# Hybrid decoder layer on one Trainium2 core: smaller first pieces, state matmuls over 128 rows, and the gate's weight parts in one tile

## The chip, the cores and the metric

The kernel runs on one core of one Trainium2 chip. The metric is the device time of one execution in microseconds (us), lower is better. A core has five engines that run their own instruction streams: TensorE (PE in the profile; its weight loads are PEld), VectorE (DVE), ScalarE (ACT), GpSimd (POOL) and SyncE (SP). SP, ACT and POOL can issue DMA transfers, each on a queue of its own. A "q" behind an engine's name in a row means its sequencer, which issues DMAs.

## The reference

One decoder layer on x of 256 tokens by 2048 features, in float32, with three residual blocks:

```python
x = x + 0.5 * swiglu(rms_norm(x, ffn1_norm), w_gate, w_up, w_down)       # 2048 -> 5632 -> 2048
h = rms_norm(x, mix_norm);  z = h @ w_in                                 # columns split among head groups
# gated linear attention (GLA), 4 heads, dk 128, dv 256, chunks of 64 tokens:
log_a = log_sigmoid((g_low @ gla_gate_up) * ... + gla_gate_bias) / 16    # g_low: 16 columns of z
#   S_c = decay_c * S_{c-1} + k_state_c^T @ v_c ;  o_c = q_c S_{c-1} + masked scores @ v_c
# dilated attention, 8 heads of 128, three causal windows merged by their denominators
x = x + concat(o_gla, o_att) @ w_out
x = x + 0.5 * swiglu(rms_norm(x, ffn2_norm), ...)
```

With 256 tokens there are four chunks, so states after chunks 0, 1 and 2 are needed.

## The kernel before

**Arithmetic.** The large products run as three matmuls in fp32r. Every operand is split into a high part (a copy rounded to fp32r, on ACT, L89) and a low part (the rest, on DVE, L90) by `split`, and `products` sums high times high (L171), low weight times high (L173) and high weight times low (L175). Activations (`hh`/`hl`, 128 tokens at a time) are the stationary operand, the weights stream by as 128x512. The small matmuls of the two attentions run in plain fp32; each of them shows as two passes in the trace.

**Weights.** All weight matrices lie in DRAM as tiles of 128x2048 (1 MB). `prepare` takes the next entry of the list `jobs`: at even k it issues the 1 MB transfer into `raw` (three buffers) on SP's queue, the very first one in four pieces of 256 KB (L148), and then splits one 128x1024 half into `wh` and `wl` (four buffers each, `WBUF`). `weights` keeps up to three tiles prepared ahead of use. One such tile is used for 12 matmuls (two token halves, two column halves, three products). The special job "low" brings 128 columns of `w_in`, from the 16 gate columns on, and splits them into two pairs of `wh`/`wl`.

**Start.** `WARM` matmuls on a zeroed tile run on TensorE first (L78). `gT` (the norms' gains, 24 KB) is loaded on ACT's queue. `first(i)` loads two k-tiles of the transposed x (`xt`, 256 KB, ACT's queue, L259) into one of four `t512` buffers, and makes `hh` (ACT, L263) and `hl` (DVE, L264) of them. `first(0)` and `first(1)` are called before the first feed-forward block, the others from within its first column pair; the rms factor itself is applied later, when results leave PSUM.

**Column pairs.** `column_pair` runs over all k tiles of two 512-column blocks of outputs and calls pieces of other work from the list `later` in between. The tile framework orders each engine's instructions by a simulated schedule, so the program's order is a guide and not the exact order.

**GLA part.** `gate_low` multiplies the "low" tiles (stationary, 128x128 of which 16 columns matter) with `hh` and `hl` (256 tokens streaming): three matmuls for each of 16 k tiles (L441 to L443). Its 16 useful rows go to `gl`, and a matmul over 16 rows with `gup` (L450) gives the gate. `decays` and `scaled` make the decay factors `e1` to `e3` and scale q and k; the end of `scaled` multiplies `kg` by the decay to the end of the chunk (L485). `gla_head` makes for chunk c = 0, 1, 2 the state `kg^T @ vg` from the 64 rows (tokens) of the chunk (L521), adds the decayed state before (L527), and then the outputs with 64-column stationary operands (L536, L539).

Of the kernel before, what the change touches and what calls it, by code (L numbers as in the profile page):

```python
# [14 lines left out]
F32 = mybir.dt.float32  # L15
# [3 lines left out]
ALU = mybir.AluOpType  # L19
# [11 lines left out]
WARM = 7  # L31
# [5 lines left out]
def layer_kernel(tc, x, xT, gains, gla_gate_up, gla_gate_bias, gla_out_norm, att_q_norm, att_k_norm,  # L37
# [6 lines left out]
    with ExitStack() as es:  # L44
# [42 lines left out]
        def split(dst_h, dst_l, src):  # L87

            nc.scalar.activation(dst_h, src, AF.Copy)  # L89
            nc.vector.tensor_sub(dst_l, src, dst_h.bitcast(F32))  # L90
# [33 lines left out]
        def wtile(name):  # L124
            return wp.tile([P, 2, 512], F32R, name=name, tag=name, bufs=WBUF)

        def prepare():
            if not jobs:
                return
            job = jobs.pop(0)  # L130
            if job == "low":
                raw = wp.tile([P, KT, P], F32, name="raw", tag="raw", bufs=3)
                nc.sync.dma_start(raw, w_low.rearrange("p (k f) -> p k f", f=P))
                got = []
                for i in range(2):
                    wh, wl = (wtile(n).rearrange("p j f -> p (j f)").rearrange("p (k f) -> p k f", f=P) for n in ("wh", "wl"))
                    split(wh, wl, raw[:, 8 * i:8 * i + 8, :])
                    got.append((wh, wl))
                ready.extend(got)
                return  # L140
            w, i, k = job
            if k == 0:
                raw = raws[0] = wp.tile([P, 2, 2, 512], F32, name="raw", tag="raw", bufs=3)
                flat = raw.rearrange("p k j f -> p (k j f)")
                parts = 1 if started else 4
                started.append(True)
                for c in range(0, 2048, 2048 // parts):
                    nc.sync.dma_start(flat[:, c:c + 2048 // parts], w[i, :, c:c + 2048 // parts])  # L148
            wh, wl = wtile("wh"), wtile("wl")
            split(wh, wl, raws[0][:, k])  # L150
            ready.append((wh, wl))

        def weights():
            while jobs and len(ready) <= AHEAD:
                prepare()
            return ready.pop(0)
# [100 lines left out]
        def first(i):  # L257
            xt = t512("xt").rearrange("p (k s) -> p k s", k=2)
            nc.scalar.dma_start(xt, xTv[:, 2 * i:2 * i + 2, :])  # L259
# [22 lines left out]
        first(0)  # L282
        first(1)
# [3 lines left out]
        with tc.tile_pool(name="mix", bufs=1, reuse_waits="tile") as mp:  # L287
# [5 lines left out]
            gup = mp.tile([RANK, 512], F32, name="gup")  # L293
# [19 lines left out]
            ld(gup, gla_gate_up)  # L313
# [121 lines left out]
            def gate_low():  # L435
                gb = acc_bank()
                for k in range(KT):
                    if k % 8 == 0:
                        wh, wl = weights()
                    h, l = wh[:, k % 8, :], wl[:, k % 8, :]  # L440
                    nc.tensor.matmul(gb[:, :S], lhsT=h, rhs=hh[:, k, :], start=k == 0, stop=False)  # L441
                    nc.tensor.matmul(gb[:, :S], lhsT=h, rhs=hl[:, k, :], start=False, stop=False)  # L442
                    nc.tensor.matmul(gb[:, :S], lhsT=l, rhs=hh[:, k, :], start=False, stop=k == KT - 1)  # L443
                gbias = t512("gbias")
                ld(gbias, gla_gate_bias.unsqueeze(0).to_broadcast([P, 512]))
                gl = mp.tile([RANK, 3 * P], F32, name="gl", tag="sc", bufs=6)
                nc.vector.tensor_copy(gl[:, :S], gb[:RANK, :S])
# [25 lines left out]

            def scaled(t):
# [10 lines left out]
                nc.vector.tensor_mul(kg[:, t, :], kg[:, t, :], er)  # L485
# [29 lines left out]
            def gla_head(h):  # L515
                st = [None]
                bs = [tp_bank(), tp_bank()]
                for c in range(3):
                    rows = slice((c % 2) * 64, (c % 2) * 64 + 64)
                    kv = bs[c // 2][:, (c % 2) * GDV:(c % 2) * GDV + GDV]  # L520
                    nc.tensor.matmul(kv, lhsT=kg[rows, c // 2, h * P:(h + 1) * P],  # L521
                                     rhs=vgv[rows, c // 2, h * GDV:(h + 1) * GDV], start=True, stop=True)
# [134 lines left out]
```

## Time and profile before

| | |
|---|---|
| median of 3 runs | 1775.6 us (1775.47 to 1775.72) |
| the profiled execution | 1776.39 us, span 1774.5 us |
| TensorE busy | 1763.4 us (99%) |
| VectorE, ScalarE, GpSimd busy | 995.3 (56%), 839.4 (47%), 372.4 us (21%) |
| bytes read from HBM | 350.35 MB, 199 GB/s over the span |

The span runs from the first to the last instruction of the profiled execution; the execution's own time lies 1.9 us above it. Matmuls are pipelined and their ends are modelled, so times between matmuls are best read from start to start.

### The profile page before, as it was taken

To read this page: it belongs to the slowest core of one execution; us is meant where nothing else is said; L and a number is where in the kernel's file an instruction comes from. 1 tells how busy PE (TensorE), PEld (TensorE's weight loads), DVE (VectorE), ACT (ScalarE), POOL (GpSimd) and SP (SyncE) were. 2 spreads that over 40 slices of the span, in tenths; PEclk is the share of its full clock that TensorE was granted. 3 is DMA by queue.
4 is the path that set the end of the run, shared out by engine and by line. 5 is a ranking of instruction groups with operands and counts; after the bars stand their busy time and mean duration, and the time that the engine had idled before them with its cause. 6 is when DMAs were issued, how large, how long until landed. Compare 5 with 4: busy or idle time off the path is not lost.

```text
span 1774.5 us, 21587 instructions
## 1 busy us (share of the span) xinstructions
PE 1763.4 (99%) x8286; PEld 1534.8 (86%) x8286; DVE 995.3 (56%) x1042; ACT 839.4 (47%) x1012; POOL 372.4 (21%) x738
## 2 busy tenths in 40 slices
PE   8999999999999999999999999999999999999999
PEld 7888888888888888888887788888888888888887
DVE  5555555555554646566655666555555555544544
ACT  6444444444444544565753455444444444444442
POOL 0333343434400001011000000333333343410000
PEclk9999999999999999999999999999999999999999
DMA  8566666666555556555444455666565656565653
GB/s 332 206 223 210 218 215 216 212 222 223 208 211 201 201 194 208 210 191 196 166 166 146 149 197 196 209 218 216 211 221 207 224 207 224 204 220 207 221 212 119
DMA packets 74648, 365.43 MB, mean 206 GB/s; under 512 B 17168, under 2 KB 30480, under 8 KB 32304
## 3 DMA queue, kind: packets, MB, share of 16 engines
q1 hardware_dynamic: 48672, 348.15, 55.0%
q0 software_dynamic: 22976, 12.73, 2.5%
q10 hardware_dynamic: 2896, 3.17, 0.6%
q8 instruction: 65, 1.06, 0.2%
q14 instruction: 39, 0.32, 0.0%
HBM read 350.35 MB, written 2.10 MB: 199 GB/s over the span
## 4 chain that ended last, share of the span: by engine, by line
PE 99%; ACT 1%; DMA 0%; DVE 0%; issue 0%; ACTq 0%
PE acc L171 32%; PE acc L173 32%; PE acc L175 32%; PE tp L85 1%; PE tp L521 0%; DMA xt<-in_xT_dram 0%; PE tp L387 0%; PE tp L536 0%; PE tp L539 0%; ACT wh L89 0%; ACT L454 0%; PE acc L441 0%; PE acc L443 0%; PE acc L442 0%; PE tp L413 0%
## 5 line engine op out<-in xcount | busy, mean ns | idle before, releaser
L90 DVE TENSOR_TENSOR wl<-raw,wh 128x1024 fp32r<-128x1024 f32 x658 | 802.8, 1224 | 713.4 <-ACT wh L89 713.2
L89 ACT ACTIVATE wh<-raw 128x1024 fp32r<-128x1024 f32 x658 | 692.1, 1056 | 864.4 <-PE acc L175 852.0
L173 PE MATMUL acc<-wl,hh 128*128 128x512 f32 x1792 | 547.6, 381 | 0.0
L175 PE MATMUL acc<-wh,hl 128*128 128x512 f32 x1792 | 543.6, 380 | 0.0
L171 PE MATMUL acc<-wh,hh 128*128 128x512 f32 x1792 | 536.6, 381 | 4.7 <-ACT wh L89 4.7
L233 POOL DMA_DIRECT2D ur<-us x704 | 344.2, 497 | 576.3 <-ACT sg L225 431.8
L171 PEld LDWEIGHTS acc<-wh,hh 128*128 128x128 f32 x1792 | 338.6, 189 | 53.6 <-ACT wh L89 5.0
L173 PEld LDWEIGHTS acc<-wl,hh 128*128 128x128 f32 x1792 | 338.6, 189 | 49.5 <-issue 2.0
L175 PEld LDWEIGHTS acc<-wh,hl 128*128 128x128 f32 x1792 | 338.4, 189 | 49.7 <-issue 2.1
L173 PE MATMUL acc<-wl,uh 128*128 128x512 f32 x704 | 212.5, 379 | 0.0
L175 PE MATMUL acc<-wh,ul 128*128 128x512 f32 x704 | 211.8, 379 | 0.0
L171 PE MATMUL acc<-wh,uh 128*128 128x512 f32 x704 | 210.6, 379 | 0.0
L175 PEld LDWEIGHTS acc<-wh,ul 128*128 128x128 f32 x704 | 133.1, 189 | 18.9
L171 PEld LDWEIGHTS acc<-wh,uh 128*128 128x128 f32 x704 | 133.0, 189 | 18.9
L173 PEld LDWEIGHTS acc<-wl,uh 128*128 128x128 f32 x704 | 133.1, 189 | 18.7
L106 POOL TENSOR_TENSOR rs<-a,mhalf 128x4 f32<-128x4 f32 (+1 forms) x12 | 17.4, 1454 | 278.7 <-DVE a L337 278.7
L307 POOL DMA_DIRECT2D rope<-in_c_rope_dram x1 | 0.7, 747 | 209.2 <-PE acc L175 209.2
L226 DVE SCALAR_TENSOR_TENSOR u<-acc,rt,sg 128x512 f32<-128x512 f32 x44 | 32.7, 744 | 0.0
L230 DVE STREAM_TRANSPOSE us<-u 128x512 f32<-128x512 f32 x44 | 31.3, 711 | 1.5
L225 ACT ACTIVATE sg<-acc,rt 128x512 f32<-128x512 f32 x44 | 29.8, 678 | 0.6
L90 DVE TENSOR_TENSOR ul<-ur,uh 128x512 fp32r<-128x512 f32 x44 | 30.1, 683 | 0.0
L106 POOL TENSOR_TENSOR rt<-ssum,mhalf 128x1 f32<-128x1 f32 x6 | 3.9, 642 | 123.1 <-DVE ssum L110 123.0
(147 smaller groups left out, 601.1 us busy)
## 6 DMA issues: line engine op xcount, KB each, us to landing
raw<-in_w_ff_dram SPq DMA_DIRECT2D x175, 1024.0 KB, 4.9
raw<-in_w_dn_dram SPq DMA_DIRECT2D x88, 1024.0 KB, 4.8
raw<-in_w_mix_dram SPq DMA_DIRECT2D x48, 1024.0 KB, 4.8
raw<-in_w_out_dram SPq DMA_DIRECT2D x16, 1024.0 KB, 4.8
ur<-us POOLq DMA_DIRECT2D x704, 16.0 KB, 3.8
xt<-in_xT_dram ACTq DMA_DIRECT2D x8, 256.0 KB, 7.0
xs<-in_x_dram SPq DMA_DIRECT2D x2, 1024.0 KB, 8.9
raw<-in_w_ff_dram SPq DMA_DIRECT2D x4, 256.0 KB, 6.0
```

What stands on the lines that cost most here:

```text
L85: nc.tensor.transpose(dst, src, ident[:n, :n])
L89: nc.scalar.activation(dst_h, src, AF.Copy)
L90: nc.vector.tensor_sub(dst_l, src, dst_h.bitcast(F32))
L106: nc.gpsimd.tensor_tensor(dst, src, mhalf[:, :src.shape[-1]], op=ALU.pow)
L171: nc.tensor.matmul(ps[j], lhsT=sh, rhs=alt(wh[:, j, :]), start=first and i == 0, stop=False)
L173: nc.tensor.matmul(ps[j], lhsT=sh, rhs=alt(wl[:, j, :]), start=False, stop=False)
L175: nc.tensor.matmul(ps[j], lhsT=sl, rhs=alt(wh[:, j, :]), start=False, stop=last and i == len(ws) - 1)
L225: nc.scalar.activation(halves(sg), ps[0], AF.Silu, scale=rt[:, t:t + 1])
L226: nc.vector.scalar_tensor_tensor(halves(u), ps[1], rt[:, t:t + 1], halves(sg), op0=ALU.mult, op1=ALU.mult)
L230: nc.vector.transpose(us.rearrange("p (q j c) -> p j q c", q=4, j=4), u)
L233: nc.gpsimd.dma_start(ur[32 * q:32 * q + 32, r * P:(r + 1) * P], us[32 * r:32 * r + 32, q * P:(q + 1) * P])
L307: ld(rv, c_rope.rearrange("(t p) f -> p t f", p=P))
```

## The change

The start: three more warm-up matmuls; x tiles go out on SP's queue, among the weights, and no longer on ACT's; the first x tile comes in two pieces of 128 KB; the first weight tile is prepared between `first(0)` and `first(1)`, and the first two weight tiles are split in two halves of 512 columns each.

The gate: a "low" tile holds the high part in columns 0 to 15 and the low part in columns 64 to 79 of one zeroed `wh` tile, so that two matmuls for a k tile (with `hh` and with `hl`) give all products, the low parts in rows 64 to 79. The product of both low parts is included too. `gup` holds its 16 rows twice, at 0 and at 64, and zeros between; the second gate matmul runs over 80 rows and so adds the two parts.

The states: `scaled` multiplies k by a column of 0 and 1 that is one in the chunk's rows (a column of the mask in `csq`), so that the other chunk's rows are zero, and writes chunk 0 into `la`'s first half, which is no longer needed, and chunks 1 and 2 in place. The state matmul then runs over all 128 rows.

```diff
-WARM = 7
+WARM = 10
@@ prepare, job "low"
                 for i in range(2):
-                    wh, wl = (wtile(n).rearrange("p j f -> p (j f)").rearrange("p (k f) -> p k f", f=P) for n in ("wh", "wl"))
-                    split(wh, wl, raw[:, 8 * i:8 * i + 8, :])
-                    got.append((wh, wl))
+                    w = wtile("wh").rearrange("p j f -> p (j f)").rearrange("p (k f) -> p k f", f=P)
+                    nc.gpsimd.memset(w.bitcast(F32), 0.0)
+                    split(w[:, :, 0:RANK], w[:, :, 64:64 + RANK], raw[:, 8 * i:8 * i + 8, 0:RANK])
+                    got.append(w)
@@ prepare
             wh, wl = wtile("wh"), wtile("wl")
-            split(wh, wl, raws[0][:, k])
+            if len(started) < 3:
+                started.append(True)
+                for j in range(2):
+                    split(wh[:, j], wl[:, j], raws[0][:, k, j])
+            else:
+                split(wh, wl, raws[0][:, k])
             ready.append((wh, wl))
-        def weights():
+        def weights(early=False):
+            if early:
+                return prepare()
@@ first
-            nc.scalar.dma_start(xt, xTv[:, 2 * i:2 * i + 2, :])
+            if i == 0:
+                for j in range(2):
+                    nc.sync.dma_start(xt[:, j, :], xTv[:, j, :])
+            else:
+                nc.sync.dma_start(xt, xTv[:, 2 * i:2 * i + 2, :])
...
         first(0)
+        weights(True)
         first(1)
@@ mixer's constants
-            gup = mp.tile([RANK, 512], F32, name="gup")
+            gup = mp.tile([64 + RANK, 512], F32, name="gup")
-            ld(gup, gla_gate_up)
+            nc.gpsimd.memset(gup, 0.0)
+            for r in (0, 64):
+                ld(gup[r:r + RANK, :], gla_gate_up)
@@ gate_low
-                        wh, wl = weights()
-                    h, l = wh[:, k % 8, :], wl[:, k % 8, :]
-                    nc.tensor.matmul(gb[:, :S], lhsT=h, rhs=hh[:, k, :], start=k == 0, stop=False)
-                    nc.tensor.matmul(gb[:, :S], lhsT=h, rhs=hl[:, k, :], start=False, stop=False)
-                    nc.tensor.matmul(gb[:, :S], lhsT=l, rhs=hh[:, k, :], start=False, stop=k == KT - 1)
+                        w = weights()
+                    nc.tensor.matmul(gb[:, :S], lhsT=w[:, k % 8, :], rhs=hh[:, k, :], start=k == 0, stop=False)
+                    nc.tensor.matmul(gb[:, :S], lhsT=w[:, k % 8, :], rhs=hl[:, k, :], start=False, stop=k == KT - 1)
...
-                gl = mp.tile([RANK, 3 * P], F32, name="gl", tag="sc", bufs=6)
-                nc.vector.tensor_copy(gl[:, :S], gb[:RANK, :S])
+                gl = mp.tile([64 + RANK, 3 * P], F32, name="gl", tag="sc", bufs=6)
+                nc.vector.tensor_copy(gl[:, :S], gb[:64 + RANK, :S])
@@ scaled
-                nc.vector.tensor_mul(kg[:, t, :], kg[:, t, :], er)
+                for c in (2 * t, 2 * t + 1)[:2 - t]:
+                    one = csq[:, 2, 63 + 64 * (c % 2):64 + 64 * (c % 2)]
+                    kz[c] = la[:, 0, :] if c == 0 else kg[:, t, :]
+                    nc.vector.scalar_tensor_tensor(kz[c], kg[:, t, :], one, er, op0=ALU.mult, op1=ALU.mult)
@@ gla_head
-                    rows = slice((c % 2) * 64, (c % 2) * 64 + 64)
-                    nc.tensor.matmul(kv, lhsT=kg[rows, c // 2, h * P:(h + 1) * P],
-                                     rhs=vgv[rows, c // 2, h * GDV:(h + 1) * GDV], start=True, stop=True)
+                    nc.tensor.matmul(kv, lhsT=kz[c][:, h * P:(h + 1) * P],
+                                     rhs=vgv[:, c // 2, h * GDV:(h + 1) * GDV], start=True, stop=True)
```

## Rows read from the trace of the kernel before

**Rows 1.** The page: busy time, share of the span and instructions of each engine, and the shares of the chain that ended last by line.

```profile
PE 1763.4 (99%) x8286; PEld 1534.8 (86%) x8286; DVE 995.3 (56%) x1042; ACT 839.4 (47%) x1012; POOL 372.4 (21%) x738
PE acc L171 32%; PE acc L173 32%; PE acc L175 32%; PE tp L85 1%; PE tp L521 0%; DMA xt<-in_xT_dram 0%; PE tp L387 0%; PE tp L536 0%; PE tp L539 0%; ACT wh L89 0%; ACT L454 0%; PE acc L441 0%; PE acc L443 0%; PE acc L442 0%; PE tp L413 0%
```

**Rows 2.** Whom TensorE waited for over the whole span, the first row: total us, times, longest us.

```profile
PE acc L171 <- ACT wh L89: 4.7, 1, 4.7
```

**Rows 3.** The timeline of the first 18 us, some of its rows: start us, us, engine, line, operation, count, and in brackets the idle time before and its releaser. A row with a count merges neighbours of one kind.

```profile
1.49 3.35 PE L78 MATMUL tp<-warm 128*128 128x128 f32 x14 [1.49 <-DVE warm L75]
7.66 0.51 ACT L263 ACTIVATE hh<-xt,gT 128x256 fp32r<-128x256 f32 x1 [4.97 <-DMA xt<-in_xT_dram]
8.47 1.04 ACT L89 ACTIVATE wh<-raw 128x1024 fp32r<-128x1024 f32 x1
9.56 2.08 PE L171 MATMUL acc<-wh,hh 128*128 128x512 f32 x4 [4.72 <-ACT wh L89]
13.99 0.65 PE L175 MATMUL acc<-wh,hl 128*128 128x512 f32 x2
14.47 1.03 PE L171 MATMUL acc<-wh,hh 128*128 128x512 f32 x4
17.07 1.03 PE L171 MATMUL acc<-wh,hh 128*128 128x512 f32 x4
```

**Rows 4.** DMA issues, each row from a narrow stretch of its own: tensors, queue, count, KB, us from issue to landing (issued at 0.74 and 5.34 us); the timeline's rows of the issues of the 1 MB transfers raw1 and raw2 and of raw3; and SP's waits in the first 45 us (total, times, longest).

```profile
gT<-in_gains_dram ACTq DMA_DIRECT2D x1, 24.0 KB, 4.6
raw<-in_w_ff_dram SPq DMA_DIRECT2D x1, 1024.0 KB, 7.4
5.34 0.81 SPq L148 DMA_DIRECT2D raw<-in_w_ff_dram  x2
12.72 0.33 SPq L148 DMA_DIRECT2D raw<-in_w_ff_dram  x1
SPq L148 <- DVE wl L90: 17.5, 5, 4.1
SPq L148 <- DMA gT<-in_gains_dram: 2.8, 1, 2.8
```

**Rows 5.** DMA traffic: all packets of the first 12 us, and of the first 30 us; two stretches of the table by windows (the last two columns are the DMA engines' busy share and GB/s); and the 88 weight loads of 1 MB for the down projections, with their median time to landing.

```profile
DMA packets 1755, 3.20 MB, mean 266 GB/s; under 512 B 283, under 2 KB 1075, under 8 KB 1603
DMA packets 3910, 10.48 MB, mean 349 GB/s; under 512 B 451, under 2 KB 2499, under 8 KB 3027
2.00:7.00 5.00, 2.84 (x14) 2.55 (x12) 0.00 (x0) 0.68 (x2) 0.00 (x0) 1.00 0.91 222
11.00:12.00 1.00, 1.00 (x4) 0.81 (x3) 1.00 (x3) 0.33 (x1) 0.00 (x0) 1.00 0.98 409
raw<-in_w_dn_dram SPq DMA_DIRECT2D x88, 1024.0 KB, 4.8
```

**Rows 6.** The timeline of TensorE at the first gate matmul and at the first weight matmul behind the 48.

```profile
826.99 0.29 PE L441 MATMUL acc<-hh,wh 128*128 128x256 f32 x1
...
832.69 0.59 PE L171 MATMUL acc<-wh,hh 128*128 128x512 f32 x2
```

**Rows 7.** The timeline of TensorE around the second gate matmul (16*128 is rows times columns of the stationary operand).

```profile
837.01 0.59 PE L173 MATMUL acc<-wl,hh 128*128 128x512 f32 x2
837.53 1.98 PE L450 MATMUL tp<-gup,gl 16*128 16x512 f32 x4
839.44 0.70 PE L175 MATMUL acc<-wh,hl 128*128 128x512 f32 x2
839.98 0.59 PE L171 MATMUL acc<-wh,hh 128*128 128x512 f32 x2
```

**Rows 8.** The timeline of TensorE around a plain fp32 matmul of full height, two passes of 512 columns.

```profile
928.47 1.02 PE L482 MATMUL tp<-la,csq 128*128 128x512 f32 x2
928.93 0.99 PE L173 MATMUL acc<-wl,hh 128*128 128x512 f32 x2
929.76 0.59 PE L175 MATMUL acc<-wh,hl 128*128 128x512 f32 x2
```

**Rows 9.** The state matmuls: all passes of line 521 (min, median, max ns, first and last start, shape) and the first line of what its weight loads waited for (us, times); then the timeline of TensorE around one visit, and around one that follows the output matmuls of L539.

```profile
L521 PE MATMUL tp<-vg,kg x24: 376/428/480, 946.8 to 995.7; 64*128 64x256 f32 x24
  issue: 3.8, 11
950.94 0.38 PE L175 MATMUL acc<-wh,hl 128*128 128x512 f32 x1
951.25 0.70 PE L521 MATMUL tp<-vg,kg 64*128 64x256 f32 x2
...
952.19 0.59 PE L171 MATMUL acc<-wh,hh 128*128 128x512 f32 x2
...
960.17 0.70 PE L521 MATMUL tp<-vg,kg 64*128 64x256 f32 x2
961.33 0.59 PE L173 MATMUL acc<-wl,hh 128*128 128x512 f32 x2
```

**Rows 10.** What lies beside: the low half of the first gate tile on DVE, GpSimd's zeroing of a 128x512 tile (group: busy us, mean ns), and its next work behind the gate's stretch.

```profile
820.51 1.23 DVE L90 TENSOR_TENSOR wl<-raw,wh 128x1024 fp32r<-128x1024 f32 x1 [1.37 <-ACT wh L89]
L505 POOL MEMSET sm<- 128x512 f32 x2 | 1.0, 522 | 2.6 <-DVE m L350 2.6
961.61 0.71 POOL L106 TENSOR_TENSOR rs<-a,mhalf 128x2 f32<-128x2 f32 x1 [151.71 <-DVE a L337]
```

More of the change, by code (lines that the diff above doesn't have):

```diff
@@ L472, in decays @@
                 nc.vector.tensor_copy(dec[:, t, :], v(e3[:, t, :])[:, :, 63])
+            kz = {}
             def scaled(t):
```

## Prediction

> **What bounds the kernel now.** I read the page's busy table and chain first: TensorE is busy 99% of the span, and 96% of the chain that ended last is the three lines of `products` [rows 1]. The table of waits then says where TensorE stood still for something else: 4.7 us, once, before its first real matmul [rows 2]. So a part of this change pays only if it lets real matmuls start earlier, removes TensorE work, or removes lost time between matmuls that a busy column hides. Time taken from ACT, DVE or POOL pays nothing. Two stretches matter: the first 17 us, and the GLA part from 827 to 1002 us.
>
> In the first 17 us [rows 3] the warm-up ends at 4.84 (1.49 + 3.35). The first `hh` waits until 7.66 for `xt`, the first weight split comes behind two of them on ACT at 8.47, and TensorE starts at 9.56. Its matmuls start 0.43 us apart up to 13.99 and 0.215 us apart later: the 1.2 and the 2.4 GHz level for 512 columns, after 4.4 us of work that followed 4.7 us of idling. Weight tile k=0 (12 matmuls) ends at 14.47, k=1 at 17.07. One tile takes 2.58 us at the higher level.
>
> **The start, costed.** I rebuild the time at which tile k=2 can run, since from there on `before` does not wait.
>
> First a price for transfers, since only early ones with small packets count. The two DMA answers hold 1755 packets and 3.20 MB in the first 12 us, of which about 10 carry traffic, and 2155 packets and 7.28 MB more in the next 18 us [rows 5]. Two equations in 16 engines' time (160 and 288 us) give 0.041 us a packet and 27.4 us a MB. Traffic starts at about 2.0, that is 1.3 us after the first issue at 0.74. A steady 1 MB (128 packets) lands 4.8 us after its issue [rows 5] and by this price moves in 2.1 us; 4.8 - 1.3 - 2.1 leaves 1.4 us from last byte to landing.
>
> Now the first matmul. `gT` landed at 0.74 + 4.6 = 5.3 [rows 4], `xt` just ahead of 7.66. After the change `xt` leads on SP in two pieces, the weight pieces follow some 0.9 us later, and `gT` keeps its place, so the first `hh` can start at about 5.3. The first weight piece has gT, ident, xt0 and itself before its end: 640 packets, 0.61 MB, (26 + 17)/16 = 2.7 us, landing at 2.0 + 2.7 + 1.4 = 6.1. Splits by halves make the first matmul wait for that one piece, and a 128x512 split should take half of 1.04 us. ACT: two `hh` take 0.8 us (7.66 to 8.47 now), to 6.1, and half a split goes to 6.7: first matmul at about 6.7. Ten warm-up matmuls in place of seven end at 1.49 + 10/7 x 3.35 = 6.28; they cost nothing, but below 6.28 nothing can start. TensorE then idles 0.4 us in place of 4.7, and I take the higher level to come before or soon after 6.7 (it came after 4.4 us of work). k=0 and k=1 end at 6.7 + 2 x 2.58 = 11.9.
>
> Then k=2, which needs the next 1 MB transfer, raw1. Ahead of its end stand xt0 to xt2, raw0 and itself, with `gT` and `ident` beside them: 2.97 MB in some 1664 packets, (68 + 81)/16 = 9.4 us. It has moved at 11.4 and lands at 12.8, where it lands now too (5.34 + 7.4) [rows 4]. Its split takes 1.04 us, so k=2 starts at about 13.8 in place of 17.07: **3.3 us**. The low half comes 1.2 us later from DVE [rows 10], and TensorE has eight matmuls that don't need it. What is late next is thus the second weight transfer, and it covers whatever is lost before it: k=0 wholly at the lower level would end k=1 near 14.
> Bounds: with the small packets (1.92 MB) at the 222 GB/s of the stretch from 2 to 7 us, and raw1 at the 409 of a later one [rows 5], it lands at 2.0 + 8.7 + 2.5 + 1.4 = 14.6 and the gain is 1.4; with no wait for raw1, from 6.28 on, k=1 ends at 11.44: 5.6.
>
> The ninth load of all seems to wait for the first: raw1 stood 2.8 us until `gT` had landed [rows 4]. In the new order that ninth is xt2, and raw1 is issued by about 5.8, long before the ring has moved what is ahead of it: no cost. SP carries nine more issues of 0.4 us, and the later x tiles wait there for their buffer with weights queued behind them; those weights wait for DVE's split in any case, up to 4.1 us [rows 4]. The issues leave ACT's queue, where nothing on the path waited for them but the x tiles themselves.
>
> **Gate parts in one tile.** 48 matmuls with 256 columns run from 826.99 to 832.69, 5.70/48 = 0.119 us each [rows 6]. 16 fall away: **1.9 us**, all of it TensorE time. The zeroing on POOL is new: 128x512 takes 0.52 us, so about 1.0 us for each of two tiles [rows 10]. It stands between the release of a buffer and the split. The cover: the low half of the first gate tile ends at 821.74 (820.51 + 1.23) for use at 826.99, 5.2 us ahead [rows 6, 10], and the splits themselves shrink from 1024 columns to 128. Without cover it would cost 1.0 us a tile. Behind them on POOL comes a reciprocal root only at 961.61 [rows 10]. `gup`'s zeroing and second load hold POOL about 1 us ahead of `rt`, which is first read when the mixer's first results leave PSUM, a column pair of 16 tiles (41 us) later, so nothing waits.
>
> **The gate's second matmul.** The 16-row matmul (four passes) runs between two 128-row ones: starts at 837.22 (second of the pair at 837.01), then 839.98 after a pair from 839.44 [rows 7]. What should four full-height fp32 passes of 512 columns take? L482 shows it: 928.47 to 929.76 holds two such passes and two fp32r matmuls, 1.29 - 0.43 = 0.86, or 0.43 a pass, and no gap around them [rows 8]. So ideal is 837.22 + 0.215 + 1.72 + 0.43 = 839.58 against 839.98: **0.4 us** if 80 rows behave like 128, 0 if like 16. No row has 80; I take 0.4. The Trainium skill (TensorEngine Tiling, Available Configurations and Key Properties) knows row tiles of 128, 64 and 32 only and says that a change of mode drains the engine; by that 80 rows are the full mode, and the sum would hold the same 0.4.
>
> **Chunk states from 128 rows.** Twelve matmuls, 24 passes on 64 rows, each a visit of its own between other work; their weight loads wait 3.8 us for "issue" in 11 times [rows 9]. One visit: 950.94 before it, 952.19 for the second fp32r matmul behind it. With a full-height fp32 matmul of 256 columns (0.43) it would be 950.94 + 0.215 + 0.43 + 0.215 = 951.80: 0.39 lost. Three of the twelve come straight behind the 64-column matmuls of L539, which keep their own switch: there 960.17 + 0.43 + 0.43 = 961.03 against 961.33, 0.30. Sum 9 x 0.39 + 3 x 0.30 = **4.4 us**. Between 0 and 4.7 (all twelve at 0.39); I take 4.4, since L482 shows no such loss. DVE, 56% busy [rows 1], gets one more 128x512 product, off the path.
> A rule speaks against this part: the Trainium skill (TensorE: Matmul & The Clock Gate, Part 3) has matmuls on different row groups run side by side, which 128 rows give up. The rows show none of it here: chunk 0 and chunk 1 stand at 946.8 and 951.25 [rows 9]. By the rule adjacent pairs would have saved four times 0.43 = 1.7 us, and the part would be worth 2.7.
>
> **Sum.** 3.3 + 1.9 + 0.4 + 4.4 = 10.0 us. The profiled execution took 1776.4 (span 1774.5); it becomes 1766.4, with a span near 1764.5. The median of the runs shown is 0.8 lower, 1775.6, so **1765.6 us**. A measurement tells 0.2%, 3.6 us, from no change.
>
> **Rivals.**
> *The start gains little.* Everything on one ring makes raw1 late, or weights wait behind an x tile. For it: raw1 is already what is late next, and small packets move slowly [rows 5]. Gain 1.4 in place of 3.3, or less: 1767.5, to 1769 at none. Chance 0.2.
> *The lost time around the states is not the 64 rows'* but comes with any change from fp32r to fp32 there. Against: L482 [rows 8]. Then 3.3 + 1.9: 1770.4. Chance 0.1.
> *The start gains all*: 5.6, so 1763.3. Chance 0.08.
> *Slower:* an x tile waiting on SP for its buffer holds back the weight transfer behind it, and TensorE starves. A raw issued at 12.72 serves k=6, at about 27.4 (17.07 + 4 x 2.58): 14.7 us ahead. A 1 MB landing (7.4) and a split (2.3) leave 5.0 us. It decides once one wait exceeds 5.0 + 10.0 = 15 us; the longest on SP there now is 4.1 [rows 4]. At a wait of 20 us: 1780. Chance 0.03.
> That the change does nothing would need the states' and the start's parts both gone: 1.9 to 2.3 us, 1773.5. Chance 0.04. My forecast keeps 0.55.
>
> **Numbers.** Range 1763 to 1769.5: the forecast, the start's both ends, and up to near the second rival. Faster by over 0.2%: 0.93 (all but the last two rivals), the same 0.04, slower 0.03.
>
> **What would show it.** First real matmul near 6.7 with no long wait before it; raw1's split near 12.8 to 13.8 and a TensorE wait ahead of it; 32 matmuls in 3.8 us for the gate; no "issue" gaps before the state matmuls and pairs 0.43 apart; L450's four passes 1.72 apart. Wrong would be gaps that stay at the states, matmuls 0.43 apart past 10 us, or new waits of TensorE for `wh` between 12 and 40 us.

## The result, and the profile after

The changed kernel takes 1766.4 us (median of 4 runs, 1765.6 to 1767.7) against 1775.7 us before: a ratio of 0.9948, interval 0.9931 to 0.9965, or 9.3 us less. The forecast was 1765.6 us, 0.8 less than that. The profiled execution of the changed kernel is the longest of the four, 1767.7 us with a span of 1765.9 us, 8.6 us below the span of before. Runs of this one program differ by up to 2.1 us; most of that seems to come from the step of the forecast that went wrong, as the experiments below suggest.

The busy row of the changed kernel's page:

```profile
PE 1757.9 (100%) x8276; PEld 1535.6 (87%) x8276; DVE 994.3 (56%) x1045; ACT 838.5 (47%) x1014; POOL 375.3 (21%) x742
```

TensorE's waits in it over the whole span (total us, times, longest us):

```profile
PE acc L179 <- ACT wh L89: 2.3, 2, 2.0
PE tp L78 <- DVE warm L75: 1.5, 1, 1.5
```

The single wait of 4.7 us [rows 2] has become one of 2.0, at another place. The timeline of the start shows where (start us, us, engine, line, operation, count, idle time before and its releaser):

```profile
4.45 0.63 ACT L89 ACTIVATE wh<-raw 128x512 fp32r<-128x512 f32 x1 [1.76 <-DMA raw<-in_w_ff_dram]
...
5.53 0.48 PE L179 MATMUL acc<-wh,hh 128*128 128x512 f32 x1
...
11.47 0.38 PE L183 MATMUL acc<-wh,hl 128*128 128x512 f32 x1
12.72 2.00 ACT L89 ACTIVATE wh<-raw 128x1024 fp32r<-128x1024 f32 x2 [1.59 <-DMA raw<-in_w_ff_dram]
13.81 2.36 DVE L90 TENSOR_TENSOR wl<-raw,wh 128x1024 fp32r<-128x1024 f32 x2 [2.13 <-ACT wh L89]
13.84 1.13 PE L179 MATMUL acc<-wh,hh 128*128 128x512 f32 x4 [1.99 <-ACT wh L89]
15.09 1.22 PE L181 MATMUL acc<-wl,hh 128*128 128x512 f32 x2
...
18.52 1.03 PE L179 MATMUL acc<-wh,hh 128*128 128x512 f32 x4
```

The first real matmul starts at 5.53, tiles k=0 and k=1 are done by 11.9, and then TensorE waits for the split of the second weight transfer, raw1. Tile k=2 starts at 13.84 and k=3 at 18.52: 4.68 us for a tile that takes 2.58 at the higher clock. The table by windows of the same execution gives the larger part of the reason (stretch, its us, busy us of PE, PEld, DVE, ACT, POOL, then the granted clock, the DMA engines' share, GB/s):

```profile
13.80:15.00 1.20, 1.13 (x4) 0.68 (x4) 1.19 (x2) 1.20 (x2) 0.00 (x0) 0.98 0.97 387
15.00:18.50 3.50, 3.41 (x8) 2.77 (x9) 3.46 (x6) 3.11 (x6) 0.00 (x0) 0.52 1.02 408
18.50:21.00 2.50, 2.50 (x13) 2.18 (x12) 2.48 (x4) 1.29 (x2) 0.00 (x0) 1.00 1.09 442
```

From 15.0 to 18.5 the granted clock is 0.52, the 1.2 GHz level, after TensorE had stood still from 11.9 to 13.8; behind it the clock is 1.00 again. The smaller part is a wait for the low half of the weights: L181 starts 15.09 - 13.84 = 1.25 us behind the first matmul of the tile, where the four matmuls ahead of it take 0.86.

The GLA part, TensorE's timeline of the changed kernel: the gate's first matmul, and the first weight matmul behind the gate [rows 6]; the 80-row matmul and its neighbours [rows 7]; one visit of a state matmul, and one that comes straight behind the output matmuls [rows 9].

```profile
825.86 0.28 PE L455 MATMUL acc<-hh,wh 128*128 128x256 f32 x1
...
829.64 0.60 PE L179 MATMUL acc<-wh,hh 128*128 128x512 f32 x2
...
834.83 0.38 PE L179 MATMUL acc<-wh,hh 128*128 128x512 f32 x1
835.04 1.88 PE L464 MATMUL tp<-gup,gl 80*128 80x512 f32 x4
836.36 0.78 PE L179 MATMUL acc<-wh,hh 128*128 128x512 f32 x1
836.98 0.59 PE L181 MATMUL acc<-wl,hh 128*128 128x512 f32 x2
...
946.17 0.38 PE L183 MATMUL acc<-wh,hl 128*128 128x512 f32 x1
946.39 0.59 PE L540 MATMUL tp<-vg,kg 128*128 128x256 f32 x2
946.63 0.57 PE L183 MATMUL acc<-wh,hl 128*128 128x512 f32 x1
947.04 0.59 PE L179 MATMUL acc<-wh,hh 128*128 128x512 f32 x2
...
954.62 0.70 PE L540 MATMUL tp<-vg,la 128*128 128x256 f32 x2
954.97 0.78 PE L179 MATMUL acc<-wh,hh 128*128 128x512 f32 x2
955.59 0.59 PE L181 MATMUL acc<-wl,hh 128*128 128x512 f32 x2
```

The gate takes 829.64 - 825.86 = 3.78 us, 1.92 less. Around the 80-row matmul, 835.04 + 1.72 (four passes of 0.43) + 0.215 = 836.98, where L181 does start: nothing is lost. A state visit is 947.04 - 946.17 = 0.87 us long, the 0.86 of the ideal. Behind the output matmuls it is 955.59 - 954.62 = 0.97 against 1.16 before.

### The profile page after: what moved, and what is told of

It is laid out like the page before. It is cut to its first block, busy times and chain, and to the rows that moved or that the text cites. A ratio compares the mean times of both kernels' runs of the same rounds, so it can differ in the third digit from the quotient of the medians.

```text
span 1765.9 us, 21578 instructions
## 1 busy us (share of the span) xinstructions
PE 1757.9 (100%) x8276; PEld 1535.6 (87%) x8276; DVE 994.3 (56%) x1045; ACT 838.5 (47%) x1014; POOL 375.3 (21%) x742
## 4 chain that ended last, share of the span: by engine, by line
PE 99%; DMA 1%; DVE 0%; ACT 0%; SPq 0%; issue 0%
PE acc L181 32%; PE acc L183 32%; PE acc L179 32%; PE tp L85 1%; DMA raw<-in_w_ff_dram 0%; PE tp L540 0%; PE tp L402 0%; PE tp L555 0%; DMA gT<-in_gains_dram 0%; PE tp L558 0%; PE acc L455 0%; PE acc L456 0%; PE tp L428 0%; PE tp L427 0%; PE tp L477 0%; PE tp L520 0%
## 5 line engine op out<-in xcount | busy, mean ns | idle before, releaser
L90 DVE TENSOR_TENSOR wl<-raw,wh 128x1024 fp32r<-128x1024 f32 (+1 forms) x658 | 800.6, 1221 | 708.9 <-ACT wh L89 708.4
L89 ACT ACTIVATE wh<-raw 128x1024 fp32r<-128x1024 f32 (+1 forms) x660 | 690.8, 1051 | 862.9 <-PE acc L183 846.3
L181 PE MATMUL acc<-wl,hh 128*128 128x512 f32 x1792 | 549.2, 381 | 0.1
L181 PEld LDWEIGHTS acc<-wl,hh 128*128 128x128 f32 x1792 | 338.7, 189 | 49.0 <-issue 1.0
L181 PE MATMUL acc<-wl,uh 128*128 128x512 f32 x704 | 212.4, 379 | 0.0
L181 PEld LDWEIGHTS acc<-wl,uh 128*128 128x128 f32 x704 | 133.1, 189 | 18.8
```

The source lines that it names most:

```text
L181: nc.tensor.matmul(ps[j], lhsT=sh, rhs=alt(wl[:, j, :]), start=False, stop=False)
```

## The experiments

Two questions were open: which part brings how much, and why tile k=2 ran so long. My theory for the second was that the clock falls after the wait for raw1; the rival was that raw1 is simply late, and by how much varies.

### The parts one at a time

Three kernels hold one part of the change each on top of the kernel before. All stand beside 26 runs of the kernel before, median 1776.2 us.

The states alone (`scaled` and the state matmul as in the change):

```diff
-                nc.vector.tensor_mul(kg[:, t, :], kg[:, t, :], er)
+                for c in (2 * t, 2 * t + 1)[:2 - t]:
...
+                    nc.vector.scalar_tensor_tensor(kz[c], kg[:, t, :], one, er, op0=ALU.mult, op1=ALU.mult)
-                    nc.tensor.matmul(kv, lhsT=kg[rows, c // 2, h * P:(h + 1) * P],
+                    nc.tensor.matmul(kv, lhsT=kz[c][:, h * P:(h + 1) * P],
```

> The kernel before with the state part alone: zeroed rows and 128-row state matmuls. The trace of the changed kernel gives 9 x 0.39 + 3 x 0.19 = 4.1 us for it. Theory (the 64-row shape costs the pause): the time falls by 4.1, to about 1771.7, and the twelve visits show no pause of the weight loads for want of an issue. Rival (the gain there came from another order of the work, or from the start): 0 to 2 us.

Measured: 1772.0 us (1771.6 to 1772.7, 10 runs), ratio 0.9976 [0.9967, 0.9985]: 4.2 us less. In its profile the weight loads of the state matmuls (busy us, mean ns | idle before, releaser) wait 1.2 us for "issue", in 3 times, where those of before waited 3.8 in 11 [rows 9]. All of it is at `la`, and three of the four visits of `la` are those behind the output matmuls:

```profile
L525 PEld LDWEIGHTS tp<-vg,kg 128*128 128x128 f32 x16 | 3.0, 190 | 0.4
L525 PEld LDWEIGHTS tp<-vg,la 128*128 128x128 f32 x8 | 1.3, 188 | 1.2 <-issue 1.2
```

The gate alone (the "low" tile, `gup` and the matmuls of `gate_low` as in the change):

```diff
+                    w = wtile("wh").rearrange("p j f -> p (j f)").rearrange("p (k f) -> p k f", f=P)
+                    nc.gpsimd.memset(w.bitcast(F32), 0.0)
+                    split(w[:, :, 0:RANK], w[:, :, 64:64 + RANK], raw[:, 8 * i:8 * i + 8, 0:RANK])
...
+            gup = mp.tile([64 + RANK, 512], F32, name="gup")
```

> The kernel before with the gate part alone: both weight parts in one tile and the second gate matmul over 80 rows. Theory: 1.9 us for 16 matmuls less, 0.4 us for the second matmul, and perhaps the 0.7 us wait for the attention scores and 0.3 us beside it that are gone in the changed kernel: 1772.6 to 1773.5. Rival (the zeroing on GpSimd delays the split): TensorE waits up to 1 us at either tile, and the gain is 0.3 to 1.3 us.

Measured: 1773.2 us (1772.1 to 1773.6, 10 runs), 0.9982 [0.9973, 0.9992]: 3.0 us less, where the two gate terms give 2.3. The rest has a place. Before, TensorE's timeline has this row in the attention's scores, with a wait of 0.68 us for VectorE:

```profile
851.19 1.58 PE L387 MATMUL tp<-kT,qT 128*128 128x128 f32 x8 [0.68 <-DVE sc L390]
```

In the profile of the gate alone L387's matmuls come in groups of four passes throughout, and the wait is gone from its table of waits (total us, times, longest):

```profile
PE acc L172 <- ACT wh L89: 4.4, 1, 4.4
PE tp L78 <- DVE warm L75: 1.5, 1, 1.5
```

The kernels with the states alone and with the start alone still have it, 0.7 us in both; the row of the latter:

```profile
PE tp L399 <- DVE sc L402: 0.7, 1, 0.7
```

So it goes away with the gate part, with which the tile framework's planner chooses another order of work.

The start alone:

```diff
-WARM = 7
+WARM = 10
...
+                    split(wh[:, j], wl[:, j], raws[0][:, k, j])
...
-            nc.scalar.dma_start(xt, xTv[:, 2 * i:2 * i + 2, :])
+                nc.sync.dma_start(xt, xTv[:, 2 * i:2 * i + 2, :])
...
+        weights(True)
```

> The kernel before with the start part alone. Theory: tile k=3 starts at 17.0 where the clock stays up after the wait for the second transfer and at 18.5 where it falls, against 19.66: a gain of 2.7 or of 1.1 us, so 1773.1 to 1774.7, with runs some 1.6 us apart. Rival (the start part brings nothing that lasts, since later waits take it back): 1775.8.

Measured: 1773.9 us (1773.3 to 1775.3, 10 runs), 0.9988 [0.9978, 0.9998]: 2.3 us less. In its profile k=2 starts at 13.62 and then runs at the lower level, as in the changed kernel. The three parts together make 4.2 + 3.0 + 2.3 = 9.5 us; the whole change was worth 9.3 in the first set of runs and 8.9 in the second (below). They add up to within these sets' difference.

### The states again on 64 rows

The changed kernel, with its mask kept and only the rows of the state matmuls cut to 64:

```diff
+                    rows = slice((c % 2) * 64, (c % 2) * 64 + 64)
-                    nc.tensor.matmul(kv, lhsT=kz[c][:, h * P:(h + 1) * P],
+                    nc.tensor.matmul(kv, lhsT=kz[c][rows, h * P:(h + 1) * P],
```

> The changed kernel with the state matmuls on the chunk's 64 rows again, all else kept, the product with the 0 and 1 column too. It changes the height of the stationary operand alone. Theory (the height is the cause): the pause at each visit is back, twelve times 0.2 to 0.4 us, 4.1 in all: about 1770.7. Rival (the other tile for chunk 0, or the order of the work): no change from 1766.6.

Measured: 1770.1 us (1769.8 to 1772.0), 0.9969 [0.9956, 0.9982], 3.7 us above the changed kernel's 1766.4. That median is from another set of runs; against the kernel before of its own set this run gains 1776.2 - 1770.1 = 6.1 us where the changed kernel gained 9.3, so the rows are worth 3.2 to 3.7 us by the medians. What the weight loads of the state matmuls waited for (us, times) is back to the same row as before:

```profile
  issue: 3.8, 11
```

With the same data, order and mask, the number of rows alone makes the pauses.

### The same kernel again, and TensorE kept busy in the wait

First the changed kernel as it is, five runs more, then the same with eight idle products of `ident` with itself between k=1 and k=2:

```diff
+        def fill(n=8):
+            fb = tp_bank()
+            for _ in range(n):
+                tc.keep_in_program_order(nc.tensor.matmul(fb[:, :P], lhsT=ident, rhs=ident, start=True, stop=True))
+        third = ahead[2]
+        ahead[2] = lambda: (fill(), third())
```

> The changed kernel, unchanged, beside the kernel before on one chip. Its four runs so far lie between 1765.6 and 1767.7 us, a spread of 2.1 us, while four runs of the kernel before lie within 0.8. Theory: TensorE waits 2 us for the second 1 MB weight transfer, and in some executions its clock falls to the lower level after that wait; tile k=2 then takes about 4.7 us in place of 2.6, 2.1 us more. So the runs should lie in two groups some 2 us apart, or spread between 1765.6 and 1767.7, and the mean granted clock of the longer ones should be below 1.000. Rival: the landing of that transfer itself varies; then the wait differs between runs and the clock does not.

> The changed kernel with eight 128x128 fp32 matmuls on the identity put behind tile k=1, into the wait for the second weight transfer; their result is not read. At the higher clock they take 8 x 0.21 = 1.7 us of a wait of 2.0. Theory (the clock falls because TensorE idles there): the granted clock stays at 1.00 through 20 us, k=2 takes 2.6 to 3.0 us from 13.8, k=3 starts near 16.8 in place of 18.5, and the runs lie close together near 1765.6 and below 1766. Rival (the transfer's landing varies, or DVE and ACT feed k=2 too slowly): k=2 stays near 4.7 us and the spread stays; or the fill delays k=2 and the time rises by up to 1.7.

The changed kernel again: 1766.9 us (1766.2 to 1768.8), 0.9951 [0.9939, 0.9964], 8.9 us below the 1775.8 of the kernel before in the same set. Its profile, span 1764.4, has the wait too, but not the slow stretch behind it:

```profile
13.89 1.13 PE L179 MATMUL acc<-wh,hh 128*128 128x512 f32 x4 [2.29 <-ACT wh L89]
15.15 0.70 PE L181 MATMUL acc<-wl,hh 128*128 128x512 f32 x2
...
16.98 1.03 PE L179 MATMUL acc<-wh,hh 128*128 128x512 f32 x4
```

and its row of the table by windows:

```profile
15.00:17.00 2.00, 1.87 (x10) 1.64 (x10) 2.00 (x4) 1.60 (x4) 0.00 (x0) 1.00 1.06 439
```

Here k=2 takes 16.98 - 13.89 = 3.09 us at a granted clock of 1.00, so the fall after the wait comes in some executions only. Over all nine runs of this kernel, the three whose mean clock is 0.999 took 1767.7, 1768.3 and 1768.8 us; the six with 1.000 took 1765.6 to 1766.9. The medians are 1768.3 and 1766.2, 2.1 us apart; a k=2 of 4.68 in place of 3.09 us makes 1.6 of them.

With the filling matmuls: 1766.3 us (1766.0 to 1767.3), 0.9946 [0.9933, 0.9960], and the mean clock is 1.000 in all five runs. That does not prove that the filling holds the clock up: six of the nine runs without it have 1.000 too, and at that rate five of five come by chance in about one case of eight ((6/9)^5 = 0.13). The filling does not make those runs shorter either, 1766.3 against the 1766.2 of the six. The expected start of k=3 near 16.8 did not come: k=2 starts at 15.00 and k=3 at 18.09, at a granted clock of 1.00. So the rival is partly right as well, since raw1's split came 1.2 us later there, though raw1 went out at 5.08 in it and at 5.05 in the first profile of the changed kernel:

```profile
13.89 2.00 ACT L89 ACTIVATE wh<-raw 128x1024 fp32r<-128x1024 f32 x2 [1.55 <-DMA raw<-in_w_ff_dram]
```

### Raw1 in two halves, with and without the filling

```diff
-                parts = 1 if started else 4
+                parts = (4 if not started else 2 if len(started) == 3 else 1)
```

> The changed kernel with the second 1 MB weight transfer issued as two of 512 KB, so that tile k=2 waits for its own half alone. At 409 GB/s the first half lands about 1.2 us ahead of the whole. Theory (this transfer is what is late): the split of k=2 starts near 11.5 in place of 12.72, TensorE waits about 0.8 us in place of 2.0, the clock stays up after the shorter wait, and the median falls by 1 us if the clock had not fallen, by 3 where it had: near 1764.6, with a small spread. Rival (small packets slow the ring, so that smaller pieces land later): the split starts at 12.7 or later and nothing is gained.

> Both: the second weight transfer in two halves, and four identity matmuls (0.85 us at the higher clock) in the remaining wait. Theory: as with the halves alone if a wait of 0.8 us does not bring the clock down, or up to 2 us better where it does; near 1764.6. Rival: the fill is in the way of k=2, some 0.5 us slower than the halves alone.

Halves: 1765.9 us (1765.5 to 1766.3), 0.9943 [0.9931, 0.9956]. Halves and four filling matmuls (`fill(n=4)`): 1766.0 us (1765.5 to 1766.2), the same ratio and interval. The forecast of 1764.6 for both was not reached. In the profile of the first the split starts at 12.43 (11.5 was expected) and k=2 at 13.54 after a wait of 1.40 us; in that of the second they start at 11.66 and at 12.77, after a wait of 0.30. Neither has a run over 1766.3. Against the changed kernel's 1766.9 in the same set both are about 1 us lower, too little for their intervals to tell apart from it; by the medians of the spans (1764.0 and 1764.2 against 1764.4) it is 0.2 to 0.4.

### The x tiles on ACT's queue, and seven warm-up matmuls

Two single steps of the start taken back in the changed kernel:

```diff
-                    nc.sync.dma_start(xt[:, j, :], xTv[:, j, :])
+                    nc.scalar.dma_start(xt[:, j, :], xTv[:, j, :])
...
-                nc.sync.dma_start(xt, xTv[:, 2 * i:2 * i + 2, :])
+                nc.scalar.dma_start(xt, xTv[:, 2 * i:2 * i + 2, :])
```

> The changed kernel with all x tiles back on ACT's queue, beside the weights and not among them; the pieces, the early split and the ten warm-up matmuls stay. Theory (all bytes share the same 16 engines, and the second weight transfer is what counts): the first matmul comes up to 2 us later, but tile k=2 still starts at 13.5 to 14.5, so the time changes by less than 1 us from 1766.6. Rival (the order on one ring is what brings the start): the first matmul near 8 to 9.5 as before the change, tile k=3 near 18 to 19.5, and the time 1 to 2 us longer, about 1768.

```diff
-WARM = 10
+WARM = 7
```

> The changed kernel with seven warm-up matmuls, as before the change. They end at 4.8 in place of 5.5 to 6.1. Theory: the first matmul needs its data until 5.5 and the wait for the second weight transfer covers the rest, so nothing changes beyond 0.3 us, even if the higher clock comes a little later. Rival (three more matmuls bridge the time to the data and so keep the higher clock): tiles k=0 and k=1 run at the lower clock up to 9 us or more; tile k=2 then starts after 13.8, and the time rises by 0.5 to 2 us.

X on ACT's queue: 1768.6 us (1767.7 to 1769.6), 0.9957 [0.9944, 0.9970], some 2 us above the changed kernel, as the rival had it. Its waits of TensorE, and then two rows of its timeline:

```profile
PE acc L179 <- ACT wh L89: 2.6, 1, 2.6
PE acc L179 <- ACT hh L275: 1.2, 1, 1.2
```

```profile
11.96 0.51 ACT L275 ACTIVATE hh<-xt,gT 128x256 fp32r<-128x256 f32 x1 [2.97 <-DMA xt<-in_xT_dram]
...
14.95 1.78 PE L179 MATMUL acc<-wh,hh 128*128 128x512 f32 x4 [2.60 <-ACT wh L89]
```

With the weights alone on SP and x beside them, x comes late and raw1 early. The first matmul starts at 6.82. Raw1, issued at 4.91, has landed 6.1 us later, at 11.0, against 12.7 in the changed kernel. But its split stands behind the third x tile on ACT, which waits 2.97 us for that tile, makes two `hh` of it and then, once DVE's `hl` ends at 13.39, issues a further x tile on its own queue (13.42); only then does the split start, at 13.84. In this profile the clock falls behind the wait too:

```profile
16.00:19.00 3.00, 3.00 (x9) 2.30 (x9) 2.54 (x5) 2.35 (x4) 0.00 (x0) 0.55 0.77 236
```

Against the first profile of the changed kernel, where the clock fell as well, k=2 starts 14.95 - 13.84 = 1.1 us later and k=3, at 19.33, 0.8. That is what the order of need on one queue, with the issues off ACT, is worth in these two profiles. The rest of the 2 us between the medians may be the clock, whose mean is 0.999 in three of these five runs and in three of nine of the changed kernel; that is too few to say that it falls more often with x on ACT's queue.

Seven warm-up matmuls: 1766.4 us (1765.8 to 1768.1), 0.9948 [0.9933, 0.9962], no difference. In its profile the matmuls of k=0 run 0.43 us apart, the clock being up only from about 9.2 us on, and k=2 still starts at 13.45: raw1's landing covers what is lost before it.

### Raw1 in halves, and the x tiles one weight tile later

```diff
-        ahead = {2 * i: (lambda i=i: first(i + 2)) for i in range(KT // 2 - 2)}
-        ahead.update({9 + 2 * t: (lambda t=t: load_x(t)) for t in range(NT)})
+        ahead = {2 * i + 1: (lambda i=i: first(i + 2)) for i in range(KT // 2 - 2)}
+        ahead.update({10 + 2 * t: (lambda t=t: load_x(t)) for t in range(NT)})
```

and `parts` as above.

> The second weight transfer in two halves, and the third x pair (xt2, 256 KB) issued behind it and not ahead of it; later x pairs move back by one tile as well. Theory (what stands on the ring ahead of the second weight transfer sets the start): by the price worked out from the trace of the kernel before, 256 packets and 0.26 MB less are (256 x 0.041 + 0.26 x 27.4)/16 = 1.1 us; the split of tile k=2 starts near 11.3, against 11.7 to 12.4 with the halves alone, TensorE waits 0.5 us or less, and the median falls by another 0.5 to 1 us, to about 1765.2. Rival (the x pair is late instead): tile k=4 waits, and the gain is lost.

Measured: 1765.5 us (1764.6 to 1767.0), 0.9942 [0.9928, 0.9956]. Its profile, span 1762.8, has no wait before k=2 at all:

```profile
10.75 1.06 ACT L89 ACTIVATE wh<-raw 128x1024 fp32r<-128x1024 f32 x1 [0.79 <-DMA raw<-in_w_ff_dram]
...
11.86 1.13 PE L179 MATMUL acc<-wh,hh 128*128 128x512 f32 x4
...
14.95 1.03 PE L179 MATMUL acc<-wh,hh 128*128 128x512 f32 x4
```

k=3 starts 2.0 us earlier than in the second profile of the changed kernel; the spans differ by 1.6. Two of its five runs are within those of the changed kernel, so that it beats it is likely and not shown. And k=2 still takes 14.95 - 11.86 = 3.09 us, at a granted clock of 1.00 and without a wait ahead of it; the last run was for those 0.5 us.

### Tile k=2 split in halves as well

On top of that version:

```diff
-            if len(started) < 3:
+            if len(started) < 5:
```

> The version with raw1 in two halves and the x tiles one weight tile later, in which tile k=2 is now also split in two halves of 512 columns. In that version's profile k=2 starts at 11.86 with no wait and takes 3.09 us to the start of k=3 (14.95) at a granted clock of 1.00, where a tile takes 2.58. Theory: the 0.5 us are TensorE waiting for the low half, which VectorE has 1.2 us after the high half, while the order that runs has only four matmuls (0.86 us) that need no low half. With half splits the first low piece is ready some 0.7 us after the first high piece, so k=2 should take 2.6 to 2.7 us, and the start of k=3 moves to about 14.4. Rival: the 0.5 us are the first matmuls' own cost behind a change of tile, and k=2 still takes 3.0 to 3.1 us. The time: 0.4 to 0.5 us less than that version's 1765.5, about 1765.0, by the theory; 1765.5 by the rival. A difference this small is read from the profile and not from the medians.

Measured: 1764.7 us (1763.8 to 1765.3, 5 runs), 0.9935 [0.9921, 0.9949]. TensorE's timeline:

```profile
12.06 1.22 PE L179 MATMUL acc<-wh,hh 128*128 128x512 f32 x4
13.12 0.38 PE L181 MATMUL acc<-wl,hh 128*128 128x512 f32 x1
...
14.85 1.03 PE L179 MATMUL acc<-wh,hh 128*128 128x512 f32 x4
```

k=2 takes 14.85 - 12.06 = 2.79 us (2.6 to 2.7 were expected), and the rest that is lost, 0.2, lies among the first four (13.12 - 12.06 = 1.06 against 0.86), whose weight loads now wait for the second high half:

```profile
12.58 0.30 PEld L179 LDWEIGHTS acc<-wh,hh 128*128 128x128 f32 x2 [0.22 <-ACT wh L89]
```

So the 0.5 us were the wait for the low half, as the theory had it: 0.3 of it is gone, and 0.2 has become a wait for the high one. raw1 landed later than in the version's other profile (its split starts at 11.38 against 10.75), and the spans are equal, 1762.8. All five runs lie below all nine of the changed kernel (1765.6 to 1768.8). The two did not run side by side, but the kernel before was no faster beside this version (1776.4) than beside the changed kernel (1775.7 and 1775.8), so this version beats both: by 1.6 us at the medians against the first set of runs of the changed kernel, by 11.7 against the kernel before in its own set.

## Why the prediction was right, and which of its steps was not

Taken at the start of k=3, which before was at 17.07 + 2.58 = 19.65 [rows 3], the terms of the two profiles of the changed kernel are:

| term | forecast | first profile | second profile |
|---|---|---|---|
| start | 3.3 | 19.65 - 18.52 = 1.1 | 19.65 - 16.98 = 2.7 |
| 16 gate matmuls | 1.9 | 1.9 | 1.9 |
| 80-row matmul | 0.4 | 0.4 | 0.4 |
| states | 4.4 | 9 x 0.39 + 3 x 0.19 = 4.1 | 4.1 |
| wait in the scores | 0 | 0.7 | 0.7 |
| sum; difference of the spans | 10.0 | 8.2; 8.6 | 9.8; 10.1 |

The three lower terms are measured in the first profile and carried over to the second. The last 0.3 to 0.4 us are put to no row. That the forecast came within 0.8 us is in part luck: the start was forecast 0.6 to 2.2 us too high and the states 0.3, and the 0.7 in the scores and these last 0.3 to 0.4, which the forecast did not have, made up for some of it.

**The start.** The step that failed is the last one, that k=2 runs on without loss from 13.8 on. What led up to it held: raw1's split started at 12.72 (forecast 12.8), k=2 at 13.84 (13.8), and the wait before it fell where "what is late next" said. That the first matmul came at 5.53 and not at 6.7 (`gT` landed 3.9 us after its issue, in place of 4.6, and half a weight split went ahead of both `hh`) brought nothing, as that paragraph said it would. The floor of 6.28 under the first matmul was wrong too: the ten warm-up matmuls ended at 5.51, since they sped up under way (20 passes in 4.02 us, where the 14 of before took 3.35). But behind the wait two things cost time. I had eight matmuls that need no low half; in the order that runs there are four, 0.86 us, and the low half's first use stands 1.26 us behind the first of them (13.89 and 15.15 in the second profile). That made k=2 3.09 us long and not 2.58 in each profile with the higher clock, 0.5 us, and the run with k=2 in halves gave 0.3 of it back. And I carried the higher clock through a wait of 2 us, although the trace of before showed that it was down after one of 4.7: another 4.68 - 3.09 = 1.6 us, in about three of nine runs of the changed kernel if the mean clock is a guide. The term should have been 3.2 - 0.5 = 2.7 with the clock kept and 2.7 - 1.6 = 1.1 without, as the two profiles have it; the mean over three such cases in nine, 2.2, is close to what the start alone measured, 2.3. The rival "the start gains little" named another cause, a late raw1; that does occur (1.2 us in the profile with the filling). Its 1.4 was not low enough, since the first profile has 1.1, but the range held. Of the signs of being wrong, matmuls 0.43 apart past 10 us did show in the first profile (the eight between 15.09 and 18.52, in 3.43 us), and pointed at the step that failed; the other, a wait for `wh` behind 12 us, was part of the forecast itself and could tell nothing.

**The gate.** Both terms came out to a tenth. 80 rows ran as 128 do, with 0.0 us lost at 835.04. The Trainium skill (TensorEngine Tiling (Array Packing), Available Configurations) lists row tiles of 128, 64 and 32, and by that 80 rows are the full mode: the trace agrees. The zeroing on POOL stayed behind its cover, for TensorE shows no wait there. What I did not foresee is that the planner would order the scores anew: a wait of 0.7 us in another place went away.

**The states.** The mechanism was right: the rival "not the 64 rows" fell with the run on 64 rows (pauses back at 3.8 us, time up by 3.2 to 3.7). From the start of k=3 to the end of the span, where the start and its clock play no part, that run takes 1768.1 - 16.53 = 1751.6 us and the second profile of the changed kernel 1764.4 - 16.98 = 1747.4, some 4.2 less, the term within 0.1. The size was 0.3 too high. Of the 0.30 us at each of the three visits behind the 64-column output matmuls, 0.11 stays (0.97 against 0.86); why it stays was not tried. The Trainium skill's rule on row groups that run side by side (TensorE: Matmul & The Clock Gate, Part 3) did not come into play; no run here puts two such matmuls next to each other, so what it would bring stays open.

**Slower.** No x tile held a weight back long enough: TensorE has no wait behind the one at k=2. Nor did the single queue cost anything: with x on ACT's queue the time was some 2 us longer, and k=3 started 0.8 later in its profile.

## What to carry to other kernels

When a wait at the start is removed, look for what is late next and then price the wait that remains twice: its length, and the stretch at the lower clock that may follow it. Lost time around matmuls with few rows does not show in a busy column, but it does from start to start of the neighbours; zero-filled full-height operands take it away, at one product more on an engine with time to spare. Short changes that alter the planner's order are worth measuring one at a time, since a wait elsewhere may come or go with them.

## What the runs showed of the hardware beyond what was expected

Behind a wait of 1.99 us the granted clock was 0.52 for some 3.5 us in one execution, and behind one of 2.29 us it stayed at 1.00 in another of the same program. It fell too behind 1.62 us with the start alone (0.51) and behind 2.60 us with x on ACT's queue. With eight small matmuls in the wait the mean clock was 1.000 in five of five runs, without them in six of nine, which does not tell the two apart. So the length of the wait alone does not decide it, and what does stays open. One thing goes along with it in the profiles: where the clock fell, the ten warm-up matmuls had taken 4.02, 4.08 and 4.18 us; where it stayed up behind a wait of over 1 us, they had taken 4.63 or 4.64 (the changed kernel again, raw1 in halves, the states on 64 rows). The two rows of the changed kernel, first and second profile:

```profile
1.49 4.02 PE L78 MATMUL tp<-warm 128*128 128x128 f32 x20 [1.49 <-DVE warm L75]
1.49 4.63 PE L78 MATMUL tp<-warm 128*128 128x128 f32 x20 [1.49 <-DVE warm L75]
```

These are six profiles, and no run varied it by itself, so it is a hint and not a cause. The profile with eight filling matmuls is one with 4.63, and so says little of what they do.

Two cautions. A mean clock of 0.999 does not by itself mean this stretch: the version with raw1 in halves and x later has it in two of five runs, 1764.9 and 1765.5 us, which are among its three shortest. And before, the rows up to 13.99 are 0.43 us apart [rows 3] while the slices of the windows at 11 us read a granted clock of 1.00 [rows 5], so near the start the spacing of the matmuls is the safer reading; with the gate alone, matmuls 0.43 apart at 11 us do read 0.50.

The landing of the same 1 MB transfer varied by about 1.2 us between executions (raw1's split at 12.72 in the changed kernel and at 13.89 in the one with the filling, with the order of issues ahead of it the same).
